# Attention mixer with 32 experts: the overflow branch ahead of the last expert, split remainders on VectorE, router logits in four column groups, LN1's g and b applied where rows are read

## The chip, the cores and the metric

One core of one Trainium2 chip runs the whole block for 256 tokens of width 1024. The metric is the device time of one execution in microseconds. The core has TensorE (PE; its weight loads are listed apart as PEld), VectorE (DVE), ScalarE (ACT) and GpSimd (POOL), and 16 DMA engines. SyncE (SP) only issues DMAs, in its own order.

## The reference, cut to what matters

```python
h = layer_norm(x, ln_in_g, ln_in_b)
# mixer: proj = h @ w_in -> differential attention (A), chunk-band attention (B), gates
m = (gate_a * (out_a @ w_branch_a) + gate_b * (out_b @ w_branch_b)) @ w_out
h = layer_norm(ALPHA * h + m, ln1_g, ln1_b)                       # LN1, ALPHA = 2 ** 0.25
logits = h @ w_router + b_router                                  # 256 x 32
top_val, top_idx = top_k(logits, 4); gate_w = softmax(top_val)
for e in range(32):                                               # the tokens that chose e
    hb = xb @ w_exp_in[e] + b_exp_in[e]                           # 1024 -> 2 x 1024
    g, u = minimum(hb[:, :1024], 7), clip(hb[:, 1024:], -7, 7)
    y = (g * sigmoid(1.702 * g) * (u + 1)) @ w_exp_out[e] + b_exp_out[e]
f = sum over a token's four experts of gate_w * y
h = layer_norm(ALPHA * h + f, ln2_g, ln2_b)                       # LN2
```

All is float32. An expert's weights are 12 MiB, so the 32 of them are 402 MB of the 439 MB that the kernel moves.

## The kernel before

**Order.** PE, DVE, ACT and POOL run their instructions in the order in which the code emits them, and so does SP from the experts on. An instruction that waits holds up all behind it on its engine.

**Mixer.** The projection with `w_in` is cut into 28 units u of 128 columns, seven groups of four in the order `W_COLS`. For each unit `prep(u + 2)` splits the weights into a rounded high part (ACT, L161) and the remainder (L162), for two halves of the rows; `multiply(u)` then does three matmuls for each 128 rows (`mm3`, L167 to L169), and `take(u)` copies what is finished out of PSUM. Between the units the dict `steps` puts the pieces of the attention: `differences(t)` (DVE, L505 to L534) forms the attention matrix of token tile t for branch A, `turn_a` transposes it, `values_a` multiplies it by v, `norm_a` and `finish_a` normalise the result (`oas`), transpose it (`oaT_ps`, L564), scale it (`oaf`, L566) and split it (`oaT`, L567). For units 5 to 9 the remainder of the second half is formed by POOL (`ON_POOL`), else by DVE.

**Routing.** The product with `w_out` (tile `mo`) makes the residual rows `r1[t]` in column halves of 512. They are transposed (`turn_r`, L761), multiplied by the router weights with g already in them (`logits_part`, L766, 16 matmuls of 32 columns for each token tile), and the mean and the scale of LN1 are put in on the 32 logits (`logits`, L769). `choose` takes the four largest, `gate_exp` and `gate_values` the softmax, `ranks` and `onehot` the place of each token in its expert's list. `h1` is LN1's result, made on DVE for three of its four 128x512 parts (L814, L818) and on ACT and POOL for the fourth (L835 to L837).

**Experts.** `for pos in range(NE)` runs 32 experts in sequence. `gather_part` or `gather_rows` picks an expert's rows out of `h1` with a one-hot matmul (tile `px`), a copy and transposes turn them into `xe`; `gemm1` multiplies `xe` by the four pieces of w1 (k = 0 to 7, two k to a piece, tile `gu`, L1123 or L1126), `act` applies the nonlinearity, `gemm2` multiplies by the two pieces of w2 (tile `py`, L1179), and `scatter` adds the weighted rows to the four PSUM accumulators `acc` with a matmul (L1193). `residual_sum` puts ALPHA times `h1` into the same accumulators (L755), in eight matmuls during the routing.

**Weights.** SP loads pieces of 2 MiB through a ring of 10 slots (`piece`); a load waits for the last matmul that read its slot. Experts 0 and 1 are fixed. From pos 2 on the expert is a number in `meta`, which `arrange(0..3)` computes: `arrange(0)` on DVE up to `by_place` (L1006 to L1010) ahead of pos 0's gemm1, `arrange(1)` inside it ahead of k = 3 (two PE products in `order_ps`, L1013 and L1016, with the DVE cast `meta`, L1014, between them), the rest ahead of k = 5 and 7.

**Branch.** Experts with more tokens than their 64 or 32 rows would take further passes (`beyond`), over 1,800 further PE instructions in the code. With this data the branch jumps over them. It stands inside the last expert's `gemm1`, ahead of k = 6, on PE, DVE, ACT and SP.

## Time and profile before

| what | value |
|---|---|
| time of three runs | 1148.89, 1145.24, 1148.49 us, median 1148.49 |
| the profiled execution | 1146.53 us, its span 1144.4 us, mean granted clock 0.946 |
| PE busy | 957.5 us (84%) |
| DVE, ACT, POOL busy | 284.9 (25%), 191.9 (17%), 55.7 us (5%) |
| DMA | 438.57 MB, mean 383 GB/s over the span |

A row of the timeline gives the start, the duration and the instructions that stand together under it; in brackets is the idle time ahead of it on its engine and what ended that. Matmul rows run into each other: PE is pipelined, so an x24 row ends where the next begins. A row of windows gives for one stretch its length, then the busy time and (x) the number of instructions of PE, PEld, DVE, ACT and POOL, the clock granted to PE (1.00 is 2.4 GHz, 0.50 is 1.2 GHz), the mean busy share of the 16 DMA engines and their rate. SP's queue rows give the moment at which a load was issued.

### The profile page before, as it was taken

The numbers are of one execution on the slowest core, as the hardware profiler recorded it, in microseconds if no ns is written. First come the engines' busy times: TensorE is split into PE (matmuls) and PEld (weight loads), VectorE is DVE, ScalarE is ACT, GpSimd is POOL, SyncE is SP. The second block draws the span as 40 slices with busy tenths as digits, with TensorE's granted clock in tenths as the row PEclk, the third lists the DMA queues.
The fourth block names the chain that finished last, engine by engine and source line by source line (L and its number), as shares of the span: only waits on it lengthen the run. The fifth ranks groups of instructions, "written<-read, shape, count | busy, mean of one in ns | idle before, by whom it ended". The sixth has DMA issues, their size and how long they took to land. (4 is left out here: it accounts for less than half of the span.)

```text
span 1144.4 us, 14111 instructions
## 1 busy us (share of the span) xinstructions
PE 957.5 (84%) x5767; PEld 427.6 (37%) x5767; DVE 284.9 (25%) x634; ACT 191.9 (17%) x413; POOL 55.7 (5%) x81
## 2 busy tenths in 40 slices
PE   9999999999999887778887869697778787878764
PEld 7988998433333222222222213131222121222211
DVE  6676667412212111111111111111111111110114
ACT  4366654211110000000000000000000000000010
POOL 3222200100010000000000000000000000000001
PEclk9999999999999999989898999898999898989987
DMA  8942569799999999999999999999999999999992
GB/s 298 384 157 77 197 280 368 281 407 427 425 413 428 429 427 427 426 426 427 427 427 426 427 427 427 424 428 428 426 427 427 425 426 426 426 427 425 427 425 100
DMA packets 52121, 438.57 MB, mean 383 GB/s; under 512 B 5006, under 2 KB 5102, under 8 KB 19538
## 3 DMA queue, kind: packets, MB, share of 16 engines
q1 hardware_dynamic: 50786, 434.29, 91.2%
q0 software_dynamic: 1120, 3.05, 0.8%
q8 instruction: 47, 0.77, 0.3%
q10 hardware_dynamic: 144, 0.26, 0.1%
q14 instruction: 24, 0.20, 0.0%
HBM read 436.14 MB, written 1.45 MB: 382 GB/s over the span
## 5 line engine op out<-in xcount | busy, mean ns | idle before, releaser
L1123 PE MATMUL gu<-w,xe 128*64 128x512 f32 x1024 | 240.2, 618 | 58.4 <-DMA w<-in_w_exp_in_dram 58.1
L1126 PE MATMUL gu<-w,xe 128*32 128x512 f32 x1024 | 152.1, 727 | 96.0 <-DMA w<-in_w_exp_in_dram 83.7
L1179 PE MATMUL py<-w,aTe 128*64 128x512 f32 (+1 forms) x1024 | 174.3, 604 | 5.5 <-ACT aTe L1166 3.1
L1123 PEld LDWEIGHTS gu<-w,xe 128*64 128x64 f32 x1024 | 74.9, 141 | 214.2 <-issue 146.4
L1151 DVE TENSOR_SCALAR a<-gu 128x512 f32<-128x512 f32 (+1 forms) x32 | 17.9, 558 | 483.4 <-PE gu L1123 254.8
L1152 ACT ACTIVATE sg<-a 128x512 f32<-128x512 f32 (+1 forms) x32 | 16.7, 523 | 534.5 <-DVE a L1151 534.5
L1126 PEld LDWEIGHTS gu<-w,xe 128*32 128x32 f32 x1024 | 31.4, 122 | 195.9 <-DMA w<-in_w_exp_in_dram 124.1
L1179 PEld LDWEIGHTS py<-w,aTe 128*64 128x64 f32 (+1 forms) x1024 | 50.3, 124 | 106.3 <-issue 90.1
L167 PE MATMUL pT<-hT_hi,w 128*128 128x256 f32 x256 | 73.9, 289 | 0.0
L168 PE MATMUL pT<-hT_lo,w 128*128 128x256 f32 x256 | 72.0, 281 | 0.0
L169 PE MATMUL pT<-hT_hi,w 128*128 128x256 f32 x256 | 72.0, 281 | 0.0
L1186 DVE COPY y<-py 128x256 f32<-128x256 f32 x32 | 13.6, 424 | 213.5 <-ACT y L1185 213.5
L1193 PE MATMUL acc<-y,st 64*128 64x512 f32 x248 | 61.6, 615 | 0.0
L162 DVE TENSOR_TENSOR w<-win,w 128x512 fp32r<-128x512 f32 (+1 forms) x65 | 49.6, 785 | 35.7 <-ACT w L161 35.7
L161 ACT CAST w<-win 128x512 fp32r<-128x512 f32 (+1 forms) x74 | 46.2, 654 | 35.5 <-PE pT L168 23.5
L1073 PE MATMUL px<-h,oh 128*32 128x256 f32 (+1 forms) x392 | 49.3, 464 | 0.7 <-ACT xe L1098 0.7
L167 PEld LDWEIGHTS pT<-hT_hi,w 128*128 128x128 f32 x256 | 48.1, 188 | 1.9 <-issue 1.3
L168 PEld LDWEIGHTS pT<-hT_lo,w 128*128 128x128 f32 x256 | 48.3, 189 | 0.0
L169 PEld LDWEIGHTS pT<-hT_hi,w 128*128 128x128 f32 x256 | 48.2, 188 | 0.1
L117 POOL TENSOR_TENSOR ln_r<-ln_ve,nhalf 128x1 f32<-128x1 f32 x6 | 3.4, 559 | 853.8 <-DVE ln_ve L115 852.8
L1185 ACT COPY y<-py 128x256 f32<-128x256 f32 x32 | 11.9, 372 | 152.5 <-PE py L1179 152.5
L1193 PEld LDWEIGHTS acc<-y,st 64*128 64x128 f32 x248 | 21.4, 186 | 34.3 <-issue 20.4
(318 smaller groups left out, 846.0 us busy)
## 6 DMA issues: line engine op xcount, KB each, us to landing
w<-in_w_exp_in_dram SPq DMA_DIRECT2D x128, 2048.0 KB, 39.1
w<-in_w_exp_out_dram SPq DMA_DIRECT2D x63, 2048.0 KB, 39.1
win<-in_w_in_dram SPq DMA_DIRECT2D x9, 2048.0 KB, 17.0
wo<-in_w_out_dram SPq DMA_DIRECT2D x2, 2048.0 KB, 7.7
win<-in_w_in_dram SPq DMA_DIRECT2D x2, 1024.0 KB
...
```

Source lines behind the costliest of these rows:

```text
L161: A.copy(hi, part)
L162: (eng[k // step % len(eng)] if isinstance(eng, tuple) else eng).tensor_tensor(lo, part, hi, op=ALU.subtract)
L167: T.matmul(dst, a[0], b[0], start=first, stop=False)
L168: T.matmul(dst, a[0], b[1], start=False, stop=False)
L169: return T.matmul(dst, a[1], b[0], start=False, stop=last)
L1073: T.matmul(px[i * w:(i + 1) * w, :], oh[:, t, :], h1[:, t, i * n:(i + 1) * n], start=(t == 0), stop=(t == NT - 1))
L1123: T.matmul(gu[i][q * w:(q + 1) * w, :], lhsT, rows[:, i, q * c:(q + 1) * c], start=first, stop=last)
L1126: T.matmul(both[q * w:(q + 1) * w], lhsT, rows[:, :, q * c:(q + 1) * c], start=first, stop=last)
L1151: V.tensor_scalar(g, gu[0], SW_LIMIT, None, op0=ALU.min)
L1152: A.activation(sg, g, AF.Sigmoid, scale=SW_ALPHA)
L1179: T.matmul(py[r:r + w, :], lhsT, w2[i][:, q, j, n * 512:(n + 1) * 512], start=(i == 0 and (m == 0 or w < CAP and m < 2)), stop=(i == 1 and ...
L1193: T.matmul(acc[t][n], st[r, t, :], y[r, :], start=False, stop=False)
```

## The change

- **Splits and steps.** `ON_POOL` is gone, so DVE forms all remainders. `finish_a(0)` now stands at unit 5 and `differences(1)` at unit 6; it was the other way round.
- **Small inputs.** The gate bias and LN1's g and b come in one tile `few` and are transposed together; `g1e` holds g and b with a column of h1 to each partition.
- **w_out and logits.** The last 512-column part of the product is done as two of 256 columns. The logits are formed by four column groups: `rT` is the moving operand and each of four groups of 32 columns takes two of the eight k, into `p4` (128x128); a copy and one matmul with four stacked identities (`fold`) sum them.
- **LN1 and the first gather.** ACT makes `h1` without g and b (`normal`). The first expert's rows are gathered already transposed (`gather_part(t)`, eight matmuls of 64 columns), and g and b are put in as `xe0` is read from PSUM, four k on DVE and four on ACT in turn. The copy `xr`, its four transposes and the copy `xe` go. `h1_finish()` then multiplies `h1` by g and adds b, in eight DVE instructions of 128x512, after `arrange(0)` and ahead of the loop.
- **Residual.** The eight `residual_sum` matmuls move from the routing to pos 8.
- **Branch.** `beyond()` stands ahead of the last expert, with four pieces of buffer in place of six; LN2's g and b have other tiles.

```diff
-        split_of[u] = split_w(src, f"w{c}_{i}", eng=(V, G) if u in ON_POOL else V)
+        split_of[u] = split_w(src, f"w{c}_{i}")
...
-    ON_POOL = range(5, 10)
...
-        5: [lambda: differences(1)],
-        6: [lambda: finish_a(0)],
+        5: [lambda: finish_a(0)],
+        6: [lambda: differences(1)],
...
+    fold = const.tile([P, NE], F32, name="fold")
+    for i in range(4):
+        V.tensor_copy(fold[i * NE:(i + 1) * NE, :], ident[i * NE:(i + 1) * NE, i * NE:(i + 1) * NE])
...
     def residual_sum(t, q):
         T.matmul(acc[t][q // 2][:, q % 2 * 256:q % 2 * 256 + 256], alpha_id, h1[:, t, q * 256:(q + 1) * 256],
-                 start=(q % 2 == 0), stop=False)
...
+    def turn_r(t, kk, part=slice(0, 4)):
+        js = range(4)[part]
+        pt = bank([P, len(js), P], f"rt{t}_{kk}_{js[0]}", "tr")
+        for i, j in enumerate(js):
+            T.transpose(pt[:, i, :], r1[t][:, (kk * 4 + j) * P:(kk * 4 + j + 1) * P], ident)
+        A.copy(rT[kk][:, part, t * P:(t + 1) * P], pt)
+    def logits_part(t, kk):
         for j in range(4):
-            T.transpose(pt[:, j, :], r1[t][:, (kk * 4 + j) * P:(kk * 4 + j + 1) * P], ident)
-        A.copy(rT[kk][:, :, t * P:(t + 1) * P], pt)
-    def logits_part(t, kk):
-        for k in range(kk * 4, kk * 4 + 4):
-            T.matmul(pl[:, t, :], rT[kk][:, k % 4, t * P:(t + 1) * P], wrg[:, k, :], start=(k == 0), stop=(k == KC - 1))
+            T.matmul(p4[j * NE:(j + 1) * NE, t, :], wrg[:, kk * 4 + j, :], rT[kk][:, j, t * P:(t + 1) * P],
+                     start=(kk == 0), stop=(kk == 1))
+    def logits_fold(t):
+        l4 = keep.tile([P, P], F32, name=f"l4_{t}", tag="t0")
+        A.copy(l4, p4[:, t, :])
+        T.matmul(pl[:, t, :], l4, fold, start=True, stop=True)
...
-    def gather_part(t, px, oh):
-        for n in range(2):
-            T.matmul(px[n * 64:(n + 1) * 64, :], oh[:, t, :], h1[:, t, n * 512:(n + 1) * 512],
-                     start=(t == 0), stop=(t == NT - 1))
-    def h1_centre(t, j, mu):
-        c = slice(j * 512, (j + 1) * 512)
-        V.scalar_tensor_tensor(h1[:, t, c], r1[t][:, c], mu, g1_b[j], op0=ALU.subtract, op1=ALU.mult)
-    def h1_finish(t, j, rs):
-        c = slice(j * 512, (j + 1) * 512)
-        V.scalar_tensor_tensor(h1[:, t, c], h1[:, t, c], rs, b1_b[j], op0=ALU.mult, op1=ALU.add)
+    def gather_part(t):
+        for k in range(KC):
+            i, j = k // 2, k % 2
+            T.matmul(px[:, k, :], h1[:, t, i * 256 + j:(i + 1) * 256:2], oh[:, t, :],
+                     start=(t == 0 and k == 0), stop=(t == NT - 1 and k == KC - 1))
+    def normal(t, m, js):
+        for j in js:
+            c = slice(j * 512, (j + 1) * 512)
+            A.activation(h1[:, t, c], r1[t][:, c], AF.Identity, bias=m[2], scale=m[1])
...
+    def h1_finish():
+        for t in range(NT):
+            for j in range(2):
+                c = slice(j * 512, (j + 1) * 512)
+                V.tensor_tensor(h1[:, t, c], h1[:, t, c], g1_b[j], op=ALU.mult)
+                V.tensor_tensor(h1[:, t, c], h1[:, t, c], b1_b[j], op=ALU.add)
...
+    def last_part(q, k):
+        c = slice(q * 256, (q + 1) * 256)
+        a, b = [m[k // 4][:, k % 4, P:2 * P] for m in mgT], ws1[k // 2 * 2][k % 2]
+        mm3(pm[1][1][:, c], a, [v[:, c] for v in b], k == 6, k == 3)
...
+    for k in (6, 7, 4, 5, 0, 1, 2, 3):
+        last_part(0, k)
+    m0 = shifted_mean(0, m0)
+    last_residual(0)
...
-    w_out_part(1, 1, 0, ws1[0])
     turn_r(0, 0)
     turn_r(0, 1)
-    w_out_part(1, 1, 2, ws1[2][:1])
-    turn_r(1, 0)
-    w_out_part(1, 1, 3, ws1[2][1:])
+    for k in (6, 7, 4, 5):
+        last_part(1, k)
+    h1 = const.tile([P, NT, D], F32, name="h1", tag="h1")
     logits_part(0, 0)
     logits_part(0, 1)
-    residual(1, 1)
-    turn_r(1, 1)
-    bn(1, 1)
+    turn_r(1, 0)
+    last_part(1, 0)
+    logits_fold(0)
+    last_part(1, 1)
+    last_part(1, 2)
+    turn_r(1, 1, slice(0, 2))
+    last_part(1, 3)
+    normal(0, m0, (0, 1))
+    logits(0, m0[0], m0[1])
+    choose(0)
+    last_residual(1)
     m1 = aggregate(1, ln1_st, "ln1")
-    logits(0, *m0)
-    choose(0)
-    normal_on_pool(h1[:, 1, 512:], r1[1][:, 512:], m1, g1_b[1], b1_b[1], "ln1_shift")
-    ex0 = gate_exp(0)
-    h1_centre(1, 0, m1[0])
     logits_part(1, 0)
+    ranks(0)
+    oh = keep.tile([P, NT, CAP], F32, name="oh0_0", tag="t2")
+    onehot(0, 0, oh, rank[:, 0, 0:1])
+    turn_r(1, 1, slice(2, 4))
     logits_part(1, 1)
-    ranks(0)
-    acc = [[bank([P, 512], f"acc{t}{n}", ("po", "sc")[t]) for n in range(2)] for t in range(NT)]
-    residual_sum(0, 0)
-    residual_sum(0, 1)
...
+    m1 = shifted_mean(1, m1)
+    logits_fold(1)
+    gather_part(0)
+    logits(1, m1[0], m1[1])
+    normal(1, m1, (0, 1))
     choose(1)
-    h1_finish(1, 0, m1[1])
-    px = bank([P, 512], "px0_0", "tr")
-    gather_part(0, px, oh)
+    stay_warm(2, "tr0")
     ranks(1)
-    residual_sum(0, 3)
     for t in range(NT):
         T.matmul(pc, ones_b, mask[:, t, :], start=(t == 0), stop=(t == NT - 1))
+    stay_warm(1, "tr0")
     onehot(0, 1, oh, rank[:, 1, 0:1])
-    residual_sum(1, 0)
-    gather_part(1, px, oh)
+    gather_part(1)
+    xe0 = [keep.tile([P, 4, CAP], F32, name=f"xe0_{i}", tag=f"t{1 - i}") for i in range(2)]
+    for k in range(4):
+        V.tensor_scalar(xe0[0][:, k, :], px[:, k, :], g1e[:, 0, k:k + 1], g1e[:, 1, k:k + 1], op0=ALU.mult, op1=ALU.add)
+        A.activation(xe0[1][:, k, :], px[:, k + 4, :], AF.Identity, scale=g1e[:, 0, k + 4:k + 5],
+                     bias=g1e[:, 1, k + 4:k + 5])
     keys = const.tile([NE, 4, NE], F32, name="keys", tag="wrg")
     V.scalar_tensor_tensor(keys[:, 0, :], pc[0:NE, :], float(NE), key_add, op0=ALU.mult, op1=ALU.add)
     V.tensor_tensor(keys[:, 1, :], pc[0:NE, :], ident[0:NE, 0:NE], op=ALU.mult)
     V.tensor_reduce(counts, keys[:, 1, :], axis=AX.X, op=ALU.add)
-    ex1 = gate_exp(1)
-    gate_values(0, ex0)
-    gate_values(1, ex1)
-    residual_sum(1, 1)
-    residual_sum(1, 2)
+    ex = [gate_exp(t) for t in range(NT)]
+    for t in range(NT):
+        gate_values(t, ex[t])
...
-            add(xe[:, k, :], w1[k // 2][:, k % 2, :].rearrange("p (i f) -> p i f", i=2), late_biases and k == 0,
+            add(xe[k // 4][:, k % 4, :] if isinstance(xe, list) else xe[:, k, :], w1[k // 2][:, k % 2, :].rearrange("p (i f) -> p i f", i=2), late_biases and k == 0,
...
-                T.matmul(acc[t][n], st[r, t, :], y[r, :], start=False, stop=False)
+                T.matmul(acc[t][n], st[r, t, :], y[r, :], start=first, stop=False)
...
+        again = [piece(f"again{i}") for i in range(4)]
...
-                        if base == bases[0]:
-                            w1, w2 = load(pos, again)
+                        e = expert(pos)
                         block = Further(pos, base)
                         block.gather()
                         block.turn()
-                        block.first(w1)
-                        block.second(w2)
+                        block.first(load_in(pos, e, again))
+                        block.second(load_out(pos, e, again))
...
+    arrange(0)
+    h1_finish()
...
-    xe = gather_T(0, 0, CAP, gathered(0, 0, px))
-    residual_sum(1, 3)
+    xe = xe0
...
         if not more:
-            last = piece("last")
-            g2, b2 = two(last[:, 0:D]), two(last[:, D:2 * D])
+            beyond()
+            g2 = two(keep.tile([P, D], F32, name="g2", tag="f2"))
+            b2 = [mid.tile([P, 512], F32, name=f"b2_{n}", tag=f"t{6 + n}") for n in range(2)]
         gated(pos, w, shifted(pos, 0), og)
         oh = onehots(pos + 1, 0, width(pos + 1), shifted(pos + 1, 0)) if more else None
-        if pos == 0:
-            arrange(0)
...
-            if not more and k == 6:
-                beyond()
...
-            scatter(st_of[:, (pos - 1) % 2], y_of[:, (pos - 1) % 2])
+            scatter(st_of[:, (pos - 1) % 2], y_of[:, (pos - 1) % 2], pos == 1)
+        if pos == 8:
+            for t in range(NT):
+                for q in range(4):
+                    residual_sum(t, q)
```

In the mixer, on DVE, units 5 to 8: `oas` is the normalised output of tile 0 ahead of its transposes, `oaf` is after them, `a_p` with `a_rs` and `rl` is `differences(1)`, `w` are remainders of units. Before:

```order
L162 TENSOR_TENSOR w_2_0_1_923<-win_632,w_2_0_0_922 128x512
L558 TENSOR_TENSOR oas_878<-oas_878,rms_r 128x512
L162 TENSOR_TENSOR w_3_0_1_956<-win_632,w_3_0_0_955 128x512
L505 RECIPROCAL a_rs_965<-a_sm_624 128x8
L530 TENSOR_SCALAR rl_967<-a_rs_965,nlam 128x4
L532 TENSOR_SCALAR a_p_1_777<-a_p_1_777,rl_967 128x256 x4
L534 SCALAR_TENSOR_TENSOR a_p_0_776<-a_p_0_776,a_rs_965,a_p_1_777 128x256 x4
L162 TENSOR_TENSOR w_0_0_1_1005<-win_634,w_0_0_0_1004 128x512
L566 TENSOR_SCALAR oaf_1017<-oaT_ps_1012,sub_432 128x512
```

The same place with the change:

```order
L162 TENSOR_TENSOR w_2_4_1_930<-win_635,w_2_4_0_929 128x512
L562 TENSOR_TENSOR oas_881<-oas_881,rms_r 128x512
L162 TENSOR_TENSOR w_3_0_1_959<-win_635,w_3_0_0_958 128x512
L162 TENSOR_TENSOR w_3_4_1_963<-win_635,w_3_4_0_962 128x512
L570 TENSOR_SCALAR oaf_973<-oaT_ps_968,sub_431 128x512
L162 TENSOR_TENSOR w_0_0_1_1005<-win_637,w_0_0_0_1004 128x512
L162 TENSOR_TENSOR w_0_1_1_1009<-win_637,w_0_1_0_1008 128x512
L509 RECIPROCAL a_rs_1012<-a_sm_627 128x8
L534 TENSOR_SCALAR rl_1014<-a_rs_1012,nlam 128x4
L536 TENSOR_SCALAR a_p_1_780<-a_p_1_780,rl_1014 128x256 x4
L538 SCALAR_TENSOR_TENSOR a_p_0_779<-a_p_0_779,a_rs_1012,a_p_1_780 128x256 x4
```

`oaf` and the remainders of unit 8 (`w_0_0`) now stand ahead of the ten instructions of `differences(1)`, and the second remainders (`w_2_4`, `w_3_4`, `w_0_1`) have joined DVE's queue.

At the start of the experts, on DVE, `og` and `oh` are gate and one-hot matrices, `keys` to `by_place` is `arrange(0)`, and the cast `meta` is the one that PE waits for in `arrange(1)`. Before:

```order
L1064 TENSOR_SCALAR og<-slots,rank,gate 128x128 x2
L1057 TENSOR_SCALAR oh_0_2533<-slots,rank 128x64 x2
L1006 TENSOR_TENSOR keys<-keys,ident 32x32
L1007 TENSOR_REDUCE key<-keys 32x1
L1008 TENSOR_SCALAR keys<-keys,key 32x32
L1009 TENSOR_REDUCE key<-keys 32x1
L1010 TENSOR_SCALAR by_place<-place,key 32x32
L1014 CAST meta<-order_ps 1x32
```

With the change:

```order
L1057 TENSOR_SCALAR by_place<-place,key 32x32
L845 TENSOR_TENSOR h_2410<-h_2410,g_0_1862 128x512
L846 TENSOR_TENSOR h_2410<-h_2410,b_0_1864 128x512
L845 TENSOR_TENSOR h_2410<-h_2410,g_1_1863 128x512
L846 TENSOR_TENSOR h_2410<-h_2410,b_1_1865 128x512
L1111 TENSOR_SCALAR og<-slots,rank,gate 128x128 x2
L1104 TENSOR_SCALAR oh_0_2599<-slots,rank 128x64 x2
L1061 CAST meta<-order_ps 1x32
```

Between `by_place` and `meta` there now stand eight instructions of `h1_finish` (the four shown come twice) and `og` and `oh`; before, `meta` followed `by_place` directly.

On PE at the last expert (`w_31`), before the branch stood between its third and fourth piece of w1:

```order
L1126 MATMUL gu_0_6183<-w_31_2_6169,xe_0_6143 32x512 x8
L1235 COMPARE_AND_BRANCH
L1235 UNCONDITIONAL_BRANCH
...
L1126 MATMUL gu_0_6183<-w_31_3_6171,xe_0_6143 32x512 x8
L1193 MATMUL acc_2443<-y,st 128x512
```

With the change it follows the second GEMM of the expert before:

```order
L1226 MATMUL py_0_6213<-w_30_0_6129,aTe_0_6206 32x512 x8
L1226 MATMUL py_0_6213<-w_30_1_6131,aTe_0_6206 32x512 x8
L1282 COMPARE_AND_BRANCH
L1282 UNCONDITIONAL_BRANCH
...
L1173 MATMUL gu_0_14482<-w_31_2_6237,xe_0_6211 32x512 x8
L1173 MATMUL gu_0_14482<-w_31_3_6239,xe_0_6211 32x512 x8
L1240 MATMUL acc_2554<-y,st 128x512
```

All four pieces of the last expert are now multiplied with no branch among them.

## Rows read from the trace of the kernel before

**Rows 1.** The page, part 2: rate of the DMA in 40 equal slices.

```profile
GB/s 298 384 157 77 197 280 368 281 407 427 425 413 428 429 427 427 426 426 427 427 427 426 427 427 427 424 428 428 426 427 427 425 426 426 426 427 425 427 425 100
```

**Rows 2.** Windows of the mixer and of the expert loop.

```profile
100.00:200.00 100.00, 100.00 (x772) 94.31 (x770) 71.51 (x110) 58.83 (x123) 12.35 (x21) 1.00 0.63 245
...
400.00:600.00 200.00, 162.14 (x888) 51.05 (x884) 27.59 (x70) 16.20 (x35) 0.00 (x0) 0.94 1.01 427
```

**Rows 3.** Timeline of SP's DMA queue: a load of expert weights.

```profile
239.78 0.33 SPq L962 DMA_DIRECT2D w<-in_w_exp_in_dram  x1
```

**Rows 4.** Timeline of PE in the mixer: units 7 and 8.

```profile
74.86 0.28 PE L167 MATMUL pT<-hT_hi,w 128*128 128x256 f32 x1
...
77.72 0.60 PE L564 MATMUL oaT_ps<-ident,oas 128*128 128x128 f32 x4
...
83.06 0.50 PE L168 MATMUL pR<-w,hT_hi 128*128 128x512 f32 x1 [1.55 <-DVE w L162]
...
84.86 0.50 PE L167 MATMUL pR<-w,hT_hi 128*128 128x512 f32 x1 [1.06 <-ACT kb L435]
```

**Rows 5.** Timelines of DVE, ACT and POOL there.

```profile
74.22 0.69 DVE L162 TENSOR_TENSOR w<-win,w 128x512 fp32r<-128x512 f32 x1 [1.64 <-ACT w L161]
...
76.56 1.79 DVE L162 TENSOR_TENSOR w<-win,w 128x512 fp32r<-128x512 f32 x1
...
82.33 0.68 DVE L162 TENSOR_TENSOR w<-win,w 128x512 fp32r<-128x512 f32 x1
...
83.70 0.62 ACT L567 CAST oaT<-oaf 128x512 fp32r<-128x512 f32 x1 [5.23 <-DVE oaf L566]
...
74.79 3.01 POOL L162 TENSOR_TENSOR w<-win,w 128x512 fp32r<-128x512 f32 x2 [1.08 <-ACT w L161]
```

**Rows 6.** Window behind these waits.

```profile
84.00:90.00 6.00, 5.14 (x20) 4.15 (x21) 2.39 (x3) 3.39 (x7) 2.75 (x2) 0.72 0.28 100
```

**Rows 7.** Timeline of PE from the routing to pos 0's second GEMM.

```profile
201.86 1.87 PE L766 MATMUL pl<-wrg,rT 128*128 128x32 f32 x16
...
211.06 1.08 PE L809 MATMUL px<-h,oh 128*64 128x512 f32 x4
...
214.35 5.37 PE L1123 MATMUL gu<-w,xe 128*64 128x512 f32 x24 [0.24 <-ACT xe L1098]
...
220.13 0.26 PE L1016 MATMUL order_ps<-by_place,ident 32*32 32x32 f32 x6 [0.27 <-DVE meta L1014]
...
220.84 3.65 PE L1123 MATMUL gu<-w,xe 128*64 128x512 f32 x16
```

**Rows 8.** Timelines of ACT and DVE there.

```profile
199.78 1.07 ACT L762 COPY rT<-rt 128x512 f32<-128x512 f32 x2 [9.51 <-PE rt L761]
...
206.30 1.28 ACT L793 ACT_TABLE_LOAD   x1
...
219.90 0.18 DVE L1014 CAST meta<-order_ps 1x32 int32<-1x32 f32 x1 [5.27 <-PE order_ps L1013]
```

**Rows 9.** Windows: the first token tile's choice, and DVE's small work behind `px`.

```profile
202.07:205.37 3.30, 3.29 (x30) 3.08 (x29) 3.02 (x14) 0.58 (x1) 0.56 (x1) 1.00 0.74 204
210.64:214.64 4.00, 3.76 (x18) 2.01 (x19) 3.62 (x21) 1.49 (x3) 0.00 (x0) 1.00 0.99 383
```

**Rows 10.** The page, part 5: DVE's half of the copy of `py`.

```profile
L1186 DVE COPY y<-py 128x256 f32<-128x256 f32 x32 | 13.6, 424 | 213.5 <-ACT y L1185 213.5
```

**Rows 11.** Timeline of PE at the last expert.

```profile
1109.84 3.31 PE L1126 MATMUL gu<-w,xe 128*32 128x512 f32 x16 [0.86 <-SPq L1235]
1119.60 3.54 PE L1126 MATMUL gu<-w,xe 128*32 128x512 f32 x16 [6.46 <-issue]
...
1126.20 3.64 PE L1179 MATMUL py<-w,aTe 128*32 128x512 f32 x32 [0.52 <-ACT aTe L1166]
```

**Rows 12.** Windows there.

```profile
1120.00:1122.00 2.00, 2.00 (x12) 0.38 (x8) 0.00 (x0) 0.00 (x0) 0.00 (x0) 0.50 0.55 225
...
1123.00:1124.00 1.00, 1.00 (x8) 0.49 (x6) 0.76 (x2) 0.26 (x1) 0.00 (x0) 1.00 0.11 45
```

More of the change, by code (lines that the diff above doesn't have):

```diff
@@ L193 @@
     rb = early.tile([HB, 2 * REL + 1], F32, name="rb")
-    bg_row = early.tile([16, P], F32, name="bg_row")
     subw = early.tile([P, 1], F32, name="subw")
@@ L315 @@
     g1p = early.tile([P, 2 * KC], F32, name="g1p")
+    g1e = const.tile([P, 2, KC], F32, name="g1e")
     wrg = const.tile([P, KC, NE], F32, name="wrg", tag="wrg")
@@ L334, in small_1 @@
     def small_1():
-        pt = bank([P, 16 + 2 * KC + 1], "small", "tr")
-        T.transpose(pt[:, 0:16], bg_row, ident[0:16, 0:16])
-        T.transpose(pt[:, 16:16 + 2 * KC], gb1, ident[0:2 * KC, 0:2 * KC])
-        T.matmul(pt[:, 16 + 2 * KC:], ones_row, l2, start=True, stop=True)
-        V.tensor_copy(bg, pt[:, 0:16])
-        V.tensor_copy(g1p, pt[:, 16:16 + 2 * KC])
-        V.tensor_copy(nlam, pt[:, 16 + 2 * KC:])
+        pt = bank([P, 16 + 4 * KC + 1], "small", "tr")
+        for h in range(2):
+            T.transpose(pt[:, h * 16:h * 16 + 16], few[:, h * P:(h + 1) * P], ident[0:16, 0:16])
+            T.transpose(pt[:, 32 + h * 8:40 + h * 8], few[0:8, h::2], ident[0:8, 0:8])
+        T.matmul(pt[:, 16 + 4 * KC:], ones_row, l2, start=True, stop=True)
+        both = pt[:, 0:32].rearrange("p (h r) -> p h r", h=2)
+        V.tensor_copy(bg.rearrange("p (r h) -> p h r", h=2), both[:, :, 8:16])
+        V.tensor_copy(g1p.rearrange("p (r h) -> p h r", h=2), both[:, :, 0:8])
+        V.tensor_copy(g1e.rearrange("p v (i h) -> p h (v i)", h=2), pt[:, 32:48].rearrange("p (h r) -> p h r", h=2))
+        V.tensor_copy(nlam, pt[:, 16 + 4 * KC:])
     row = early.tile([1, 2, NE], F32, name="row")
@@ L837, in normal_on_pool @@
         G.tensor_tensor(dst, dst, b, op=ALU.add)
-    ln1_st = const.tile([P, NT, 2, 6], F32, name="ln1_st", tag="ln1_st")
+    ln1_st = [const.tile([P, 2 + 2 * t, 6], F32, name=f"ln1_st{t}") for t in range(NT)]
     in_order = ExitStack()
@@ L862 @@
     residual(1, 0)
-    bn(0, 1)
+    bn(0, 2, 2)
     m0 = aggregate(0, ln1_st, "ln1")
-    w_out_part(1, 1, 6, ws1[6])
-    h1 = const.tile([P, NT, D], F32, name="h1", tag="h1")
-    for j in range(2):
-        h1_centre(0, j, m0[0])
-    for j in range(2):
-        h1_finish(0, j, m0[1])
-    w_out_part(1, 1, 4, ws1[4])
+    p4 = bank([P, NT, P], "p4", "po")
+    px = bank([P, KC, CAP], "px0_0", "po")
+    def last_part(q, k):
+        c = slice(q * 256, (q + 1) * 256)
+        a, b = [m[k // 4][:, k % 4, P:2 * P] for m in mgT], ws1[k // 2 * 2][k % 2]
+        mm3(pm[1][1][:, c], a, [v[:, c] for v in b], k == 6, k == 3)
@@ L976, in load_out, with load @@
         return w2
-    def load(pos, tiles=None):
+    def load(pos):
         e = expert(pos)
-        return load_in(pos, e, tiles and tiles[:4]), load_out(pos, e, tiles and tiles[4:])
+        return load_in(pos, e), load_out(pos, e)
     gb2 = const.tile([3 * NE, P], BF16, name="gb2")
@@ L1186, in results, with scatter @@
         V.tensor_copy(y[:, 256:], py[:, 256:])
-    def scatter(st, y):
+    def scatter(st, y, first=False):
         for t in range(NT):
@@ L1232, in beyond @@
     def beyond():
-        again = [piece(f"again{i}") for i in range(6)]
+        again = [piece(f"again{i}") for i in range(4)]
         with tc.If(n_beyond > 0, preferred_fallthrough_block=False):
@@ L1314 @@
     y, st = y_of[:, (NE - 1) % 2], st_of[:, (NE - 1) % 2]
-    bs = const.tile([P, NT, 2, 6], F32, name="ln2_st", tag="ln1_st")
+    bs = [const.tile([P, 2, 6], F32, name=f"ln2_st{t}", tag=f"ln1_st{t}") for t in range(NT)]
     results(y, py)
@@ L1320 @@
             T.matmul(acc[t][n], st[r, t, :], y[r, :], start=False, stop=True)
-    r2 = last[:, 2 * D:].rearrange("p (t n c) -> p t n c", t=NT, n=2)
+    r2 = piece("r2")[:, 0:2 * D].rearrange("p (t n c) -> p t n c", t=NT, n=2)
     m = []
```

41 lines of the change are left out of this document (24 added, 17 removed).

## The prediction

> **What bounds the kernel now.** I read the page's DMA rates first. From the ninth slice on, up to the last, they stand at 407 to 429 GB/s, and at 424 or more in nearly all [rows 1]. PE is busy for 162 of 200 us there, the DMA engines for all of it (share 1.01) [rows 2]. So the experts run at the pace of their weights: a piece of 2 MiB lasts 2.097 MB / 427 GB/s = 4.9 us, an expert of six pieces 29.5 us, and PE has 19% of that, 5.6 us, left over in each. Work added or removed inside the stream moves nothing. Three things can move the end: when the stream becomes steady, its bytes (unchanged), and what follows its last byte.
>
> The stream becomes steady with SP's load at 239.78 [rows 3]: its slot comes free with the first half of pos 0's second GEMM, the loads ahead of it have run out by then (slice nine ends at 257 us and has 407 where the next has 427), and later loads are issued well ahead. This gate follows from PE: gemm1 of pos 0 restarts at k = 3 at 220.84 [rows 7], and 18.9 us of PE work without a gap worth naming stand between. I call 220.84 the restart. Before it PE is full from 100 to 200 us [rows 2], so what the mixer saves reaches the gate whole.
>
> **Mixer, splits and steps.** PE waits 1.55 us for DVE's remainder (83.06) and 1.06 us for `kb`, which stands on ACT behind the cast `oaT` [rows 4, 5]. Both come from DVE: its remainder at 76.56 takes 1.79 us beside POOL's splits, and the next one starts only at 82.33, after `differences(1)`; alone it takes 0.68 [rows 5]. Then the granted clock is 0.72 over 84 to 90 us [rows 6], which loses 6 x 0.28 = 1.7 us. With the change, `oaf` and the remainders of unit 8 are ahead of `differences(1)` and none of these waits is left: -1.55 - 1.06 - 1.7 = -4.3.
>
> Against it stands a new wait. The transposes `oaT_ps` ran at 77.72, behind the matmuls of unit 6, which began at 74.86 [rows 4]; now they are ahead of them, and need `oas`. DVE gets there at 74.22 + two remainders and one product of 0.69 each = 76.3 [rows 5]. So PE waits from 74.86 to 76.3, 1.4 us. Mixer: -4.3 + 1.4 = **-2.9**. Bounds: -4.3 (`oas` is there in time) and -1.2 (the new wait brings a slow stretch of 1.7 of its own).
>
> **Routing.** PE does more ahead of its last `mo`: the eight logits matmuls of token tile 0, half of 1.87 us, = 0.94 [rows 7]; a fold and two transposes, some 0.5; more weight loads from halving the columns, some 0.4; and it waits for two copies `rT`, 1.07 us together [rows 8], whose buffer holds a split of w_out until just before. That is +2.9, at 202.07 + 2.9 = 205.0. Behind it, tile 0's way from residual to mask took 3.30 us [rows 9]; tile 1's has 256 columns left in two 0.69 us operations, -0.5, so 2.8. Rank and one-hot, some 1.2, and eight gather matmuls, each with a 128x128 weight load, some 2.4, end `px` at 211.4, where it ended at 212.14 before (211.06 + 1.08) [rows 7]. In this stretch POOL's two operations on `h1` and the copy and transposes behind `px` go too. Bounds of the end of `px`: 210.5 and 212.6.
>
> **From `px` to the restart.** This is where the change adds most. PE starts gemm1 about 2.7 us after `px`, where it was 2.2 (214.35), has 5.4 us of work for k = 0 to 2 [rows 7], and then needs the cast `meta`. Before, DVE had been idle for 5.27 us when that came [rows 8]. Now it is behind:
> - eight reads of `px` for `xe0`, in turn on DVE and ACT, about 0.29 each: 2.35;
> - the small work that stood in 210.64 to 214.64 and is still there, `og` and `oh` too: 4.0 [rows 9];
> - the wait for the softmax's exponentials: ACT can load its table (1.28 us [rows 8]) only behind `xe0`, then two of 0.32: some 1.5;
> - `h1_finish`, eight 128x512 operations at 0.68 [rows 5]: 5.4 (bounds 4.9, at the 0.60 between starts of such a pair, and 5.9);
> - `meta` to the restart: 0.94, as from 219.90 to 220.84.
>
> Sum 14.2, so the restart is at 211.4 + 14.2 = 225.6, **+4.8**. Who waits: PE, and through it the loads whose slots k = 3 and k = 5 free, and the gate.
>
> The eight reads of `px` are taken one after the other because every copy of `py` is: DVE's half always waits for ACT's, 213.5 us of its idle time ending so [rows 10]. The Trainium skill, PSUM — Partial Sum Buffer, in its terms table, says that two engines must not touch one PSUM bank at once, reads against reads included; the row agrees. Without that rule the reads would go in pairs, the sum would be 1.2 us smaller.
>
> **Clock behind the new gap.** From 211.4 + 2.7 + 5.4 = 219.5 to 224.7 or so PE idles for over 5 us. At the last expert an idle time of 6.46 us [rows 11] is followed by a clock of 0.50 to some 1123 [rows 12], 3.3 us that lose 1.65; the small idles of the mixer cost 1.7. I take **+1.5**, bounds 0 and 2.3.
>
> Gate: -2.9 + 4.8 + 1.5 = **+3.4**. Of this nothing is absorbed, since the loads ahead of it are late by the same.
>
> **Tail.** Before, PE stands at the branch for 6.46 us up to 1119.60 although k = 6 and 7 have been loaded since about 1114.7; gemm1 then takes 3.54 us at half speed, and `py` runs 1126.20 to 1129.84 [rows 11]. The DMA's last bytes come at about 1124.2 (busy share 0.11 in 1123:1124) [rows 12]. With the branch ahead of the last expert, gemm1 ends at 1116.7 to 1118.3 (as the clock is), scatter and transposes by 1121, and the second GEMM has only its last piece's matmuls behind the DMA: half of 3.64, so 1126.0 against 1129.84: **-3.9**. The branch's own 6.46 us lie where PE would wait for data anyway, 5.6 us of them in the expert, and the rest is caught up before the fourth piece. Bounds: -4.4, and -1 if slow matmuls stand at the end. The rest up to the span's end, 14.6 us of LN2 and stores, stays.
>
> The Trainium skill, Runtime: NRT & Kernel Launch, "Instruction fetch mechanics", says that a taken branch out of the fetched pages waits for a DMA of the target page; it speaks against any gain from moving it, since the fetch is paid wherever it stands. The 6.46 us at the branch agree; by the rule alone the tail would be the same, by the rows it goes under a wait.
>
> **At nothing.** `residual_sum` at pos 8: six of the matmuls took 1.54 us in the routing, so some 2 us in an expert with 5.6 to spare; without that cover it would cost 2. The `few` transposes and `g1e`: four more small operations at the start, under the first weight loads. LN2's other buffers: no operation more.
>
> **Sum.** +3.4 at the gate, which shifts the whole stream, and -3.9 behind it: **-0.5**. The profiled execution took 1146.53 us (span 1144.4 and 2.1 around it), so 1146.0 by it; the runs' median is 1148.49, 2.0 above that execution, so 1148.0 on the median.
>
> **Rivals.**
> - *The stall is shorter and the tail is the gain.* `px` ends at 210.5, the exponentials are not waited for (-1.5), the clock stays full: the restart is at 220.84 + 4.8 - 0.9 - 1.5 - 2.9 = 220.3, the gate about where it was, and -0.5 - 3.9 gives 1144.1. For it: every term there is an estimate from neighbours. Against it: `h1_finish` alone is longer than the 5.27 us that DVE had to spare. 27%.
> - *The clock takes more than the branch gives back (slower).* The place is PE's new gap ahead of k = 3, and the one ahead of `oaT_ps`. With slow stretches behind both (mixer -1.2, +2.3 at k = 3) and `px` at 212.6, the gate is at -1.2 + 6.0 + 2.3 = +7.1; less 3.9 that is +3.2, and with half of the last matmuls slow (+1.8) +5.0: 1153.5. It decides from a gate over 7.3 us late. For it: both idles of the trace that are followed through had a slow stretch. Against: five estimates must all go one way. 16%.
> - *The branch's wait is not covered.* If fetching its target takes longer beside the full stream, or DVE and ACT come out of theirs later, gemm1 of the last expert ends behind the DMA as before and the tail gives only 1: +2.4, 1150.9. For it: the wait was 6.46 us in a stretch where the DMA was still full. 14%. The rule of the Trainium skill's Runtime: NRT & Kernel Launch, named above, would bring about this case.
> - *The forecast*, within 0.3% of before: 43%.
>
> **How the numbers follow.** Three runs of before lie 0.3% apart, 3.4 us, about what a measurement can tell from no change. Faster by more (below 1145.0): the first rival, 27%. Within: forecast and third rival, 57%. Slower by more (above 1151.9): the second, 16%. The range takes in the first rival but for its best half and the second's near end: 1143.5 to 1152.3.
>
> **What would show it.** In the trace after: no remainder on POOL, the matmuls of unit 9 at about 86.5 where they were at 89.4; an idle of 5 us or so on PE ahead of the second `order_ps`, ended by DVE `meta`, with eight `h` operations of 0.68 just before on DVE; the load that was at 239.78 now near 243; no "issue" idle between pieces of the last gemm1, and `py` ending 2 us behind the DMA. A restart before 222 or after 228, a clock of 1.00 throughout 220 to 230, or a last `py` over 3 us behind the DMA would make the forecast wrong in that step.

## The result, and the profile after

The changed kernel takes 1154.3 us in the median of four runs (1153.23 to 1155.66), against 1146.97 for the kernel before in its four (1145.24 to 1148.89): a ratio of 1.0067, 95% interval 1.0046 to 1.0089. It is slower by 7.7 us, where 1148.0 was forecast for a median of 1148.49 and the range ended at 1152.3. The profiled span went from 1144.4 to 1151.5, +7.1, and three numbers make that up. The load that was issued at 239.78 [rows 3], the gate of the prediction, now comes at 247.35:

```profile
247.35 0.33 SPq L1009 DMA_DIRECT2D w<-in_w_exp_in_dram  x1
```

That is +7.6. From there to the end of the last microsecond in which the DMA engines were busy for more than a twentieth (1124 before, 1135 after) it was 884.2 us and is 887.6: +3.4. From there to the span's end it was 20.4 and is 16.5: -3.9. The gate is late, the stream is slower, the tail is shorter. One run each of e1 and e14 below (1262.8 and 1239.3 us, at a clock of 0.71 and 0.72 over the whole run) is left out of the medians.

The timeline of PE, from the mixer's new wait to the restart at k = 3, shows where the gate went. Compare [rows 4, 7].

```profile
76.30 0.66 PE L568 MATMUL oaT_ps<-ident,oas 128*128 128x128 f32 x4 [1.17 <-DVE oas L562]
...
89.11 1.95 PE L548 MATMUL oa<-va,aT 128*128 128x128 f32 x16
...
197.44 0.91 PE L775 MATMUL p<-rT,wrg 128*32 128x128 f32 x16 [0.68 <-ACT rT L770]
...
202.16 0.44 PE L769 MATMUL rt<-ident,r 128*128 128x128 f32 x2
...
203.34 0.41 PE L775 MATMUL p<-rT,wrg 128*32 128x128 f32 x4 [0.40 <-ACT rT L770]
204.17 0.41 PE L781 MATMUL pl<-fold,l 128*128 128x32 f32 x2 [0.42 <-ACT l L780]
...
208.79 3.51 PE L826 MATMUL px<-oh,h 128*128 128x64 f32 x16
215.48 7.38 PE L1170 MATMUL gu<-w,xe 128*64 128x512 f32 x24 [3.18 <-issue]
...
226.30 0.28 PE L1063 MATMUL order_ps<-by_place,ident 32*32 32x32 f32 x6 [3.29 <-DVE meta L1061]
...
227.07 5.00 PE L1170 MATMUL gu<-w,xe 128*64 128x512 f32 x16
```

The mixer's `oa` is 3.2 us earlier than in the kernel before:

```profile
92.27 1.95 PE L544 MATMUL oa<-va,aT 128*128 128x128 f32 x16
```

All of that and more is lost by 212.3, where `px` is done (212.14 before). The 24 matmuls of k = 0 to 2 take 7.38 us where they took 5.37 [rows 7], and then PE waits for `meta`. The restart is at 227.07 instead of 220.84.

The windows (length, busy times, granted clock, DMA share, GB/s, as above) show the clock at 1.2 GHz for the whole of 206 to 219, and the stream at 424 GB/s; the last row is the kernel before, 426:

```profile
206.00:219.00 13.00, 9.52 (x41) 6.87 (x42) 3.96 (x22) 3.43 (x7) 0.00 (x0) 0.50 0.73 267
300.00:1060.00 760.00, 619.88 (x3478) 195.81 (x3476) 102.33 (x265) 61.45 (x133) 6.50 (x17) 0.93 1.01 424
```

```profile
300.00:1060.00 760.00, 616.28 (x3464) 194.32 (x3464) 103.50 (x267) 61.70 (x134) 6.53 (x17) 0.94 1.01 426
```

DVE's timeline begins with tile 1's last residual and goes on to its mask. Behind `px` it reads as the prediction listed it: `xe` in turns with ACT, then the small work, then `h`, then `meta`.

```profile
201.69 0.41 DVE L908 SCALAR_TENSOR_TENSOR r<-hr,mo 128x256 f32<-128x256 f32 x1
...
204.62 0.25 DVE L784 SCALAR_TENSOR_TENSOR lg<-rows,ln_mv,pl 128x32 f32<-128x32 f32 x1 [0.73 <-PE pl L781]
...
205.91 0.18 DVE L794 TENSOR_SCALAR mask<-rep 128x32 bf16<-128x32 f32 x1
...
212.34 0.34 DVE L956 TENSOR_SCALAR xe<-px,g1e 128x64 f32<-128x64 f32 x1 [3.94 <-PE px L826]
213.22 0.34 DVE L956 TENSOR_SCALAR xe<-px,g1e 128x64 f32<-128x64 f32 x1 [0.54 <-ACT xe L957]
...
217.31 0.19 DVE L812 TENSOR_TENSOR ex<-ex,mask_f 128x32 f32<-128x32 f32 x1 [1.59 <-ACT ex L808]
...
219.94 0.67 DVE L845 TENSOR_TENSOR h<-h,g 128x512 f32<-128x512 f32 x1
...
224.63 0.69 DVE L846 TENSOR_TENSOR h<-h,b 128x512 f32<-128x512 f32 x1
...
226.08 0.17 DVE L1061 CAST meta<-order_ps 1x32 int32<-1x32 f32 x1
```

ACT makes two copies on tile 1's way from that residual to its logits:

```profile
201.51 1.52 ACT L833 ACTIVATE h<-r,ln_shift,ln_r 128x512 f32<-128x512 f32 x2
202.93 0.35 ACT L770 COPY rT<-rt 128x256 f32<-128x256 f32 x1
203.85 0.27 ACT L780 COPY l<-p 128x128 f32<-128x128 f32 x1 [0.57 <-PE p L775]
```

At the last expert (compare [rows 11]) PE meets the branch ahead of the biases, and the wait of 6.45 us stands there. A second wait of 2.56 us, put down to issue too, follows between the first two k (1118.76); the prediction expected none, and e6 and e7 below have none there. Both are caught up: the last matmuls wait for their piece of w2 (through SP's queue) and end 1 us behind the DMA.

```profile
1113.33 0.62 PE L1173 MATMUL gu<-be,sel_pl 96*32 96x512 bf16 x4 [6.45 <-issue]
...
1125.13 3.64 PE L1173 MATMUL gu<-w,xe 128*32 128x512 f32 x32
...
1135.27 1.06 PE L1226 MATMUL py<-w,aTe 128*32 128x512 f32 x8 [0.73 <-SPq L1282]
```

### The profile page after: what moved, and what is told of

Read it like the earlier page. It is cut to its first block, busy times and chain, and to the rows that moved or that the text cites. A ratio compares the mean times of both kernels' runs of the same rounds, so it can differ in the third digit from the quotient of the medians.

```text
span 1151.5 us, 14256 instructions
## 1 busy us (share of the span) xinstructions
PE 961.6 (84%) x5823; PEld 429.8 (37%) x5823; DVE 286.1 (25%) x654; ACT 194.9 (17%) x421; POOL 45.9 (4%) x74
## 5 line engine op out<-in xcount | busy, mean ns | idle before, releaser
L1170 PE MATMUL gu<-w,xe 128*64 128x512 f32 x1024 | 237.4, 611 | 59.6 <-DMA w<-in_w_exp_in_dram 56.4
L1173 PE MATMUL gu<-w,xe 128*32 128x512 f32 x1024 | 157.1, 748 | 85.0 <-DMA w<-in_w_exp_in_dram 82.3
L1240 PEld LDWEIGHTS acc<-y,st 64*128 64x128 f32 x248 | 21.3, 186 | 33.6 <-issue 20.5
```

The source lines that it names most:

```text
L1170: T.matmul(gu[i][q * w:(q + 1) * w, :], lhsT, rows[:, i, q * c:(q + 1) * c], start=first, stop=last)
L1173: T.matmul(both[q * w:(q + 1) * w], lhsT, rows[:, :, q * c:(q + 1) * c], start=first, stop=last)
L1240: T.matmul(acc[t][n], st[r, t, :], y[r, :], start=first, stop=False)
```

## The experiments

All times are medians with the ratio to the kernel before, measured beside it, and its 95% interval. The kernel before took 1144.9 to 1147.0 us in the five sets of runs, so a difference between two medians of different sets is known to some 2 us.

| kernel | median us | ratio to before |
|---|---|---|
| changed kernel | 1154.3 | 1.0067 (1.0046 to 1.0089) |
| e5, before + mixer part | 1142.05 | 0.9976 (0.9966 to 0.9986) |
| e6, before + branch ahead | 1142.75 | 0.9976 (0.9966 to 0.9986) |
| e7, before + both | 1138.99 | 0.9942 (0.9924 to 0.9961) |
| e1, changed, `h1_finish` later | 1150.17 | 1.0037 (1.0016 to 1.0057) |
| e2, changed, PE kept busy | 1152.33 | 1.0057 (1.0037 to 1.0077) |
| e8, e1 and e2 | 1145.43 | 0.9997 (0.9987 to 1.0008) |
| e10, e1 and `px` in two banks | 1146.32 | 1.0005 (0.9992 to 1.0019) |
| e9, e1 and old slot addresses | 1148.04 | 1.0024 (1.0012 to 1.0037) |
| e12, all four mends | 1139.29 | 0.9963 (0.9949 to 0.9977) |
| e14, e7, slots 64 bytes off | 1142.05 | 0.9971 (0.9956 to 0.9987) |
| e13, e12, slots aligned | 1135.06 | 0.9916 (0.9899 to 0.9932) |
| e11, e7, slots aligned | 1132.44 | 0.9894 (0.9874 to 0.9914) |

The profiled executions, cut at the gate and behind the last microsecond in which the DMA engines were busy for more than a twentieth (so the two last columns are known to 1 us each):

| kernel | gate | gate to DMA end | DMA end to span end |
|---|---|---|---|
| before | 239.78 | 884.2 | 20.4 |
| changed | 247.35 | 887.6 | 16.5 |
| e5 | 237.34 | 883.7 | 17.8 |
| e6 | 242.00 | 884.0 | 16.0 |
| e7 | 236.91 | 884.1 | 16.4 |
| e1 | 243.16 | 887.8 | 15.9 |
| e2 | 247.70 | 887.3 | 16.3 |
| e8 | 238.23 | 887.8 | 15.8 |
| e10 | 241.47 | 887.5 | 16.1 |
| e9 | 246.30 | 884.7 | 15.6 |
| e12 | 237.04 | 884.0 | 16.6 |
| e14 | 236.52 | 886.5 | 17.1 |
| e13 | 238.90 | 879.1 | 16.6 |
| e11 | 236.44 | 877.6 | 16.4 |

**The parts that gain (e5, e6, e7).** The mixer's edit is the one shown above (`ON_POOL` away, steps 5 and 6 swapped); the branch's is, in the kernel before:

```diff
         if not more:
-            last = piece("last")
-            g2, b2 = two(last[:, 0:D]), two(last[:, D:2 * D])
+            beyond()
+            g2 = two(keep.tile([P, D], F32, name="g2", tag="f2"))
...
-            if not more and k == 6:
-                beyond()
```

> The kernel before with the mixer part alone (all remainders on VectorE, finish_a(0) ahead of differences(1)). Theory: the gate comes 3.2 us earlier, the branch stays where it was: 1142.4. Rival (POOL's splits had been hiding work, or the last expert's branch eats the gain): 1145.5.

> The kernel before with the branch ahead of the last expert (and the buffers that this needs), nothing else. Theory (the tail gives 3.9 us, as the two profiles say from the DMA's end to the span's end, 20.2 and 16.3 us): 3.9 us faster than before, 1143. Rival (the branch's wait beside the full stream slows the stream itself, since the changed kernel's weights ran at 425 where 427 GB/s were before): rate 425 in its windows and no gain.

> The kernel before with the splits on VectorE, finish_a(0) ahead of differences(1), and the branch ahead of the last expert: the change without its routing part. Theory: mixer -3.2 at the gate (unit 9's values at 89.11 instead of 92.27), branch -3.9 at the tail: 7.1 us faster than before, 1140. Rival (the mixer's gain does not reach the gate): 1143, as with the branch alone.

Each alone gives about 2.8 us (1145.4 x 0.0024), where 3.1 and 3.9 were expected of them; together they give 6.6 (0.0058), which is near the 7.1 expected. In e6 the time from the gate to the DMA's end is 884.0 us, where it was 884.2, so the branch's wait does not slow the transfers as far as 1 us can tell. The branch's idle time, 6.38 us, is caught up before the end: the last matmuls wait for data again.

```profile
1103.83 0.62 PE L1126 MATMUL gu<-be,sel_pl 96*32 96x512 bf16 x4 [6.38 <-issue]
...
1126.30 1.06 PE L1179 MATMUL py<-w,aTe 128*32 128x512 f32 x8 [0.56 <-SPq L1235]
```

So the whole loss lies in the routing part: 1154.3 against 1139.0 of e7, 15 us. The other experiments take that apart.

**`h1_finish` off the way to the restart (e1).**

```diff
     arrange(0)
-    h1_finish()
...
-        gated(pos, w, shifted(pos, 0), og)
-        oh = onehots(pos + 1, 0, width(pos + 1), shifted(pos + 1, 0)) if more else None
+        if pos:
+            gated(pos, w, shifted(pos, 0), og)
+            oh = onehots(pos + 1, 0, width(pos + 1), shifted(pos + 1, 0)) if more else None
...
+            if pos == 0 and k == 3:
+                h1_finish()
...
+                gated(0, w, shifted(0, 0), og)
+                oh = onehots(1, 0, width(1), shifted(1, 0))
```

The tiles that `gated` writes are made there too, behind `h1_finish`, since their slots come free with it.

> The changed kernel, but h1_finish and the og and oh behind it stand after arrange(1), so that the cast meta follows by_place directly on DVE. Theory (DVE's queue holds the restart): meta no longer waits for 6.1 us of DVE work, PE's restart at k = 3 comes when k = 0 to 2 are done, 223 + 1.1 = 224.1 instead of 227.07, and without the 3.3 us gap the slow stretch 226.4 to 229.5 (1.3 us lost) goes too: gate load 4.3 us earlier than 247.35, time about 1150. Rival (the half clock from 206 to 219.7 is all of it): the gate moves by under 1.5 us, time 1153 or more.

The median fell by 4.1 us (3.4 by the two ratios), near the 4.3 expected; `meta` comes at once and PE has no gap:

```profile
223.03 0.21 PE L1060 MATMUL order_ps<-by_place,own_index 32*1 32x32 f32 x2
223.51 0.26 PE L1063 MATMUL order_ps<-by_place,ident 32*32 32x32 f32 x6 [0.27 <-DVE meta L1061]
```

**PE's short waits filled (e2), and both (e8).**

```diff
+    pw = bank([P, P], "pw", "sc")
+
+    def warm(n):
+        for _ in range(n):
+            T.matmul(pw, ident, ident, start=True, stop=True)
...
+    warm(3)
     logits_part(0, 0)
...
         A.copy(l4, p4[:, t, :])
+        warm(2)
...
+    warm(2)
     logits_part(1, 1)
...
     gather_part(1)
+    warm(11)
```

> The changed kernel with idle 128x128 products put into PE's short waits of the routing (3 ahead of tile 0's logits, 2 ahead of each fold and of the last logits, 11 behind the last gather). Theory (the short waits from 197 to 204, once filled by residual_sum, bring the clock down at 205.96): the granted clock stays 1.00 from 200 to 222, the gathers and gemm1's k = 0 to 2 go at full speed (6.0 us instead of 5.9 + 7.4 in all, px 1.7 us earlier), restart 1.7 us earlier, time about 1152.5. Rival (the clock falls for another reason, or the added products cost what they save): clock 0.50 as before somewhere in 205 to 220, time 1154 or more.

> Both mends of the changed kernel at once: h1_finish behind arrange(1) and products in PE's waits. Theory (DVE's queue and the clock are two separate costs): counted from the first transposes rt, where the two stretches start, the gate load stood at +53.0 us in the changed kernel, +48.6 with the first, +51.5 with the second; with both the second gap of 5.3 us on PE goes as well, and it stands at about +46, time about 1147.5. Rival (they are one cost, the gap ahead of k = 3): +48 to +49, time as with h1_finish moved alone, 1150.

In e2 the clock is 1.00 through 200 to 222 (0.69 in the changed kernel), the last gather takes 2.07 us instead of 3.51, k = 0 to 2 take 5.37 instead of 7.38, and the gap ahead of `meta` is 5.30 us, since DVE's queue is as long as before. Behind that gap stands a slow stretch of some 6.8 us (in the last window), and from the restart (226.44) to the gate it is 21.3 us, where e1 and e8, which have no gap, take 18.95:

```profile
200.00:222.00 22.00, 19.17 (x151) 14.11 (x143) 11.70 (x52) 7.91 (x16) 1.10 (x2) 1.00 0.66 241
224.00:231.00 7.00, 5.07 (x20) 1.74 (x22) 2.35 (x11) 0.00 (x0) 0.00 (x0) 0.52 0.18 77
```

```profile
209.56 2.07 PE L827 MATMUL px<-oh,h 128*128 128x64 f32 x16
...
225.63 0.33 PE L1073 MATMUL order_ps<-by_place,ident 32*32 32x32 f32 x6 [5.30 <-DVE meta L1071]
```

So each hides a part of the other: 4.1 and 2.0 us alone, 8.9 together (by the ratios 3.4, 1.1 and 8.0). In e1 the restart still stands behind k = 0 to 2 at half clock, and in e2 the gap takes up what the clock gave. From the first transposes `rt` (194.14) e8's gate is 44.1 us away, against 53.0 in the changed kernel; +46 had been expected. The two are separate costs: neither mend takes the other's away.

**`px` in two banks (e10).**

```diff
-    px = bank([P, KC, CAP], "px0_0", "po")
+    px = [bank([P, 4, CAP], f"px0_{i}", ("po", "sc")[i]) for i in range(2)]
```

> h1_finish behind arrange(1), and px in two PSUM banks, the four k that DVE reads in one and the four of ACT in the other. Theory (the eight reads go one after the other, 3.3 us, because they share a bank): four pairs in about 1.7 us, and what follows on DVE 1.6 us earlier; but with h1_finish gone the restart hangs on PE's k = 0 to 2, which start behind the reads, so it comes 1.6 us earlier too: 1149. Rival (the reads wait for each other for another reason): 3.3 us as before and 1150.4.

The turns are gone. DVE's four reads take 1.10 us together and ACT's 1.29, with no wait among them:

```profile
212.80 1.10 DVE L956 TENSOR_SCALAR xe<-px,g1e 128x64 f32<-128x64 f32 x4 [2.23 <-PE px L826]
```

```profile
214.57 1.29 ACT L957 ACTIVATE xe<-px,g1e 128x64 f32<-128x64 f32 x4 [7.14 <-PE px L826]
```

The reads of DVE begin, at 212.80, while the products for the second bank still run (the last of them starts at 214.05), and PE goes on without a wait, where e1, as the changed kernel, has one of 3.18 at this place:

```profile
214.40 7.00 PE L1170 MATMUL gu<-w,xe 128*64 128x512 f32 x24
```

The profiled gate came 1.7 us earlier than e1's, as much as expected, although PE's transposes `rt` began 1.6 later in this execution (196.22 against 194.60): from there to the gate it is 3.3 less. The median is 3.9 us below e1's, with intervals of some 2 us on either side. The two banks are worth the whole wait, and not the 1.6 that the longer reads cost.

**Where the weight slots lie (e9, e11, e14).** In the built program the ring's ten slots lie, in bytes beyond a multiple of 512, at 288 (five), 256 (three) and 480 (two) in the kernel before, and at 64, 32 and 480 in the changed one, whose small tiles take 224 bytes less ahead of them.

e9 is e1 with these 224 bytes put back as an unused tile, so that its slots lie as those of the kernel before:

```diff
+    pad = const.tile([P, 56], F32, name="pad")
+    V.memset(pad, 0.0)
```

e11 is e7 with three unused tiles and `ones_row` in another pool, so that all ten slots lie at a multiple of 512:

```diff
-    ones_row = const.tile([1, P], F32, name="ones_row")
+    pad = const.tile([P, 56], F32, name="pad")
...
+    ones_row = early.tile([1, P], F32, name="ones_row")
...
+    pad_mid = mid.tile([P, 8], F32, name="pad_mid")
...
+    V.memset(pad_right.tile([P, 120], F32, name="pad_r"), 0.0)
```

e14 is e11 with all ten slots 64 bytes on:

```diff
-    pad = const.tile([P, 56], F32, name="pad")
+    pad = const.tile([P, 72], F32, name="pad")
...
-    V.memset(pad_right.tile([P, 120], F32, name="pad_r"), 0.0)
+    V.memset(pad_right.tile([P, 104], F32, name="pad_r"), 0.0)
```

> h1_finish behind arrange(1), and an unused 224-byte tile that puts the weight ring's slots at the SBUF addresses that they have in the kernel before (the changed kernel has them 224 bytes lower). Theory (where the slots lie sets the stream's rate: 424 GB/s over 300 to 1060 us in all three kernels with the routing change, 426 in the three without): 426 GB/s, and the 865 us of stream 0.4% shorter, 3.5 us less than h1_finish moved alone: 1147. Rival (the rate falls for another reason, such as what is on PE and ACT beside it): 424 GB/s and 1150.

> The kernel before with the mixer part and the branch ahead of the last expert, and with small unused tiles that put all ten slots of the weight ring at multiples of 512 bytes (before: five at 288, three at 256 and two at 480 beyond one). Theory (the stream's rate depends on where the slots lie, and whole multiples are best): above 426 GB/s; 1 GB/s is 2 us, so below 1139.0. Rival (the rate has nothing to do with the slots): 426 and 1139.0.

> The aligned kernel with all ten weight slots moved by 64 bytes, so that each lies 64 beyond a multiple of 512. It tells what of the address matters. If whole multiples of 512 bytes do: 426 GB/s or less and 1139 or more, where the aligned one has 429 and 1132.4. If a multiple of 64 is enough: 429 and 1132.4.

Windows of the stream in e9, e11 and e14, in this order:

```profile
300.00:1060.00 760.00, 617.46 (x3486) 196.22 (x3482) 102.33 (x265) 61.40 (x133) 6.51 (x17) 0.94 1.01 426
```

```profile
300.00:1060.00 760.00, 616.71 (x3494) 194.72 (x3488) 103.33 (x267) 62.79 (x136) 6.52 (x17) 0.94 1.01 429
```

```profile
300.00:1060.00 760.00, 610.62 (x3461) 192.16 (x3454) 103.17 (x267) 61.80 (x134) 6.56 (x17) 0.94 1.01 425
```

e9 has the rate of the kernel before with the changed kernel's work, so the address is the cause. Its median is 2.1 us under e1's and not 3.4. Its profiled gate was 3.1 later: 1.5 stand before `rt` already (196.12 against 194.60), and its slow stretch lasts to 223.5, e1's to 219.4; whether that holds for its other runs is not known. e11 is the fastest of all, 13.2 us or 1.06% under the kernel before, with nothing but addresses changed over e7; e14 takes that back with 64 bytes.

**All mends (e12, e13).** e12 joins e1, the added products (into `px`'s second bank, and six of `stay_warm` behind the last gather in place of eleven), the two banks and e9's padding; e13 is e12 with e11's slots (`fold` moved out of the way).

> The whole change with its four costs taken out: h1_finish behind arrange(1), products in PE's waits, px in two banks, and the weight slots at the addresses of the kernel before (224 bytes of padding). Theory (these four are all that the routing part lost): gate load at 238.23 - 1.6 = 236.6, where the kernel before with the mixer and the branch parts alone has 236.91, stream 426 GB/s, time 1139, the same as that one. So the routing part itself would be worth nothing. Rival (something else in it still costs, or it does gain): over 1141, or under 1137.

> The same, with all ten weight slots at multiples of 512 bytes. Theory (address and routing are separate): 429 GB/s, time 1132.5, as the aligned kernel without the routing part. Rival: an interaction, 1136 or more.

e12's gate is at 237.04, e7's at 236.91, and the medians are 0.3 us apart (by the ratios 2.4, with intervals that overlap): mended, the routing part shows neither a loss nor a gain that these runs can tell (the mends themselves were not tried on the old routing). e13 is 2.6 us over e11. In the profiled execution its gate is 2.5 later, and most of that comes from the program's start: from 10 to 20 us its clock is 0.66, and the mixer's `oa` begins at 91.14 where e11 has 89.00. That also stood in e2 (0.52, 91.04), e9 (0.74, 90.50) and e10 (0.66, 91.01); what decides it was not tried, and neither was whether it stands in the runs without a profile. An interaction of address and routing is not excluded.

## Why the prediction was wrong

Two terms failed: the end of `px`, 3.8 us later than forecast, and the pace of the stream, 3.4 us, which had no term. Either alone would have left the time inside the range: 1148.0 and 3.8 is 1151.8, with 3.4 it is 1151.4.

- **Mixer: right.** -2.9 forecast, -3.2 measured at `oa`, with the new wait of 1.4 at 1.17 and no slow stretch behind it.
- **Last `mo`: right.** 205.0 less 2.9 = 202.1 forecast; tile 1's last residual starts at 201.69.
- **`px`: wrong, the first failing step.** 211.4 less 2.9 = 208.5 forecast, 212.3 measured, +3.8. Even the upper bound, 212.6 less 2.9, was passed. I took 2.8 us from residual to mask; it took 4.5 (201.69 to 206.2, in e2 at full clock as well). The row was misread: in the 3.30 us of [rows 9] the residual is tile 1's and the choice behind it tile 0's, whose logits did not need that residual, while tile 1's own logits were formed only later:

```profile
202.07 0.69 DVE L705 SCALAR_TENSOR_TENSOR r<-hr,mo 128x512 f32<-128x512 f32 x1 [2.16 <-PE mo L169]
...
203.83 0.24 DVE L769 SCALAR_TENSOR_TENSOR lg<-rows,ln_mv,pl 128x32 f32<-128x32 f32 x1
```

```profile
204.21 1.94 PE L766 MATMUL pl<-wrg,rT 128*128 128x32 f32 x16
```

So the way from a tile's own residual to its logits was not in the sum. With the change it is transposes, a copy, products, a copy and the fold, one behind the other from 202.16 to 204.6 (PE waits of 0.40 and 0.42, DVE's 0.73 above). The `h` operations that stand ahead of `rT` on ACT cost only some 0.3 of it (the transposes end at 202.60, the copy starts at 202.93). That is +1.7. The rest is the clock, +2.5: from the mask to the end of `px` 3.6 us were forecast, e2 takes 3.6 at 1.00, and the changed kernel 6.1 at 0.50. The last `mo` came 0.4 early.
- **The clock: right in kind, wrong in place and size.** I put one slow stretch behind the gap at `meta`, 1.5 us. It is there (the restart to the gate takes 20.28 us instead of 18.94, +1.3; in e2 it costs 2.3), but a longer one comes before it, from 206 to some 219.6. It has no such gap ahead of it: PE's longest wait from 186 us up to there is the 0.68 at 197.44. e2, e8, e12 and e13, with PE's waits filled, have 1.00 through this stretch; the changed kernel, e1, e9 and e10, without, have 0.50 for 10 to 17 us. So filling them is enough to keep the clock at 2.4 GHz. `residual_sum`, which I moved "at nothing" because pos 8 has room, had been standing among them: I priced where it went and not what it left. Whether its absence alone brings the stretch on was not tried; e5, e6, e7 and e11, which have it in place, have a shorter one (last section), so it is not the only cause.
- **`px` to the restart: right.** 14.2 forecast, 14.8 measured: `xe` 3.3 instead of 2.35, the wait for exponentials 1.59 (1.5), `h1_finish` 5.3 (5.4). The Trainium skill, PSUM — Partial Sum Buffer, terms table, says that two engines must not use one PSUM bank at once, and e10 agrees so far as it goes: on one bank the reads take turns, on two they don't. What reads at once on one bank would do, no run here shows.
- **The stream: wrong, a term left out.** "Its bytes (unchanged)" is true, but its pace is not: +3.4 us, 424 instead of 426 GB/s, from slots that moved by 224 bytes (e9). Nothing in the trace of before could price it; the addresses of the built program could have raised it.
- **Tail: right in mechanism, its size less sure.** -3.9 forecast, -3.9 between the two profiles, and the branch's wait is covered. But the tail of the old place is itself 20.4 us in the kernel before and 17.8 in e5, which has the branch there too, so the pairs of profiles give 4.4 (e6 against before) and 1.4 (e7 against e5). As measured alone (e6), the branch gives 2.7 with an interval of 1.6 to 3.9.

The forecast gate was +3.4 and is +7.6; with +3.4 of stream the rival that ended slower was nearest (it gave 1153.5), though by half of its mechanism: `px` was late, and by more than it took. The slow stretch behind the mixer's wait that it needed did not come.
